# A hybrid decoder layer in one launch: another order of transfers, norms and splits in the opening

## The chip, the cores and the metric

The kernel runs on one core of a Trainium2 chip. Times are device microseconds (us) of that core for one execution of the whole program. The engines are named as in the profile: PE (TensorE, with its weight loads as PEld), ACT (ScalarE), DVE (VectorE), POOL (GpSimd) and SP (SyncE, which issues most of the transfers); "q" behind an engine's name is its sequencer or its DMA queue.

## The reference, cut to what matters

One layer over 512 tokens of width 1024, all in float32:

```
u    = rms_norm(x, attn_pre_norm)
proj = u @ w_in            # q, k, v, gate, beta, decay of group A; q, k, v of group B
mix  = concat(gated_delta_rule(...), block_attention(...)) @ w_out
h    = x + rms_norm(mix, attn_post_norm)
h    = h + rms_norm(relu(rms_norm(h, mlp_pre_norm) @ w_up)**2 @ w_down, mlp_post_norm)
out  = h + sigmoid(h @ w_ple_gate) * (p @ w_ple)
```

`p` is 512 x 256 and `w_ple` 256 x 1024. The change concerns the beginning: the product `p @ w_ple`, which depends on nothing else, the first norm, and the first product of `u`.

## The kernel before, in words

Tokens are tiled by 128 (four tiles, t = 0 to 3), the width by 128 as well (eight slices, k = 0 to 7). A float32 product is done as three products of the faster type float32r: every operand is split into a high part (a cast on ACT) and a low part (a subtraction on DVE), and `mm3` (L187 to L191) multiplies high by high, high by low and low by high. So each operand that comes from memory costs one transfer, one pass on ACT and one on DVE before PE can use it.

The opening runs, in the order of the source:

- Transfers of `p_in` (two halves, k = 0 and 1), of `wl_in` (w_ple in four pieces, from ACT's queue), of x tile 0 and of the identity (L124 to L130).
- Three products of a tile of zeros, `warm`, into `pwarm` (L132 to L136), and an ACTIVATE on one column of that tile (L137), the first one in the source, whose function needs the table load.
- Memsets of `half` and `root` on POOL, and `pad_l`, a tile that only takes up room (L146 to L150).
- The splits of `p` and of the first half of `wl` (`part_of`, L232 to L234), then `embed(0)` (L236 to L246): for k = 0, 1 and four token tiles one `mm3` each, 24 products in all, whose four results are copied out of PSUM as `pls` and stored to the DRAM tile `ple`, to be read at the very end of the kernel. The splits of the second half of `wl` follow (L247).
- The norm row `nw0`, from ACT's queue (L249), and the four loads of `wv`, the weight for the token-major projections, 256 rows x 520 columns each, split as they arrive (`load_chunk` and `load_w`, L158 to L177); the raw buffers are three, those of the high and low parts four. The loads of x tiles 1 to 3 stand between them (L251 to L257).
- For each token tile the norm (L261 to L270): a square with a running sum on ACT (L264), the root on POOL (L154, L155), the scaling to `u` on DVE (L267), eight transposes on PE into `ut` (L212) and their split into `uTh` and `uTl` (L203, L204). Behind tile 0 stands `embed(1)`, the other 24 products.

Then the pool `e` of the opening is closed, and the pool `g` of the next phase reuses its memory, each tile of it waiting for the tiles that it lies on. The `wv` products come next (L279 to L288): token tiles 0 and 1 in two column halves each, over k, then tiles 2 and 3, 192 products in all; `mov` and `ba` take their results. After them the first convolution product (`pc`, in `proj_conv`) and everything else follow.

The order in which an engine runs its instructions is not the order of the source alone: the build lays out each engine's list by rank, which is the place in the source, and by the time at which its own model has the operands ready. Each engine then works through its list strictly in order. Of the transfers issued from SP and ACT eight can be under way; the issue of a ninth waits for one to land.

## Time and profile before

| | |
|---|---|
| median of 3 runs | 696.66 us (695.54 to 699.62) |
| profiled execution, its own time | 695.17 us |
| its span in the trace | 693.4 us |
| PE busy | 678.2 us, 98% of the span |
| DVE, ACT, POOL busy | 438.6, 324.0, 48.7 us |
| moved by DMA | 79.24 MB, 114 GB/s on the mean |

A row of the trace tells when an instruction began and how long it lasted; in brackets stands the time for which its engine had been idle, and what ended that. A matmul's end is modelled, so the distance between two starts is the better measure of its cost. A transfer is shown by its issue; the time from there to landing stands in the list of transfers. The rows that the prediction uses stand in their own section below.

### The profile page before, as it was taken

To read this page: it belongs to the slowest core of one execution; us is meant where nothing else is said; L and a number is where in the kernel's file an instruction comes from. 1 tells how busy PE (TensorE), PEld (TensorE's weight loads), DVE (VectorE), ACT (ScalarE), POOL (GpSimd) and SP (SyncE) were. 2 spreads that over 40 slices of the span, in tenths; PEclk is the share of its full clock that TensorE was granted. 3 is DMA by queue.
4 is the path that set the end of the run, shared out by engine and by line. 5 is a ranking of instruction groups with operands and counts; after the bars stand their busy time and mean duration, and the time that the engine had idled before them with its cause. 6 is when DMAs were issued, how large, how long until landed. Compare 5 with 4: busy or idle time off the path is not lost.

```text
span 693.4 us, 9002 instructions
## 1 busy us (share of the span) xinstructions
PE 678.2 (98%) x3418; PEld 563.2 (81%) x3418; DVE 438.6 (63%) x687; ACT 324.0 (47%) x598; POOL 48.7 (7%) x91
## 2 busy tenths in 40 slices
PE   8999999999999999999999999999999999999897
PEld 5998888888877768789888888888888888688786
DVE  4748889367676656675385456956678758535532
ACT  6536343433466655545265644444435344523311
POOL 1401100000011100230000000000000000032100
PEclk9999999999999999999999999999999999999999
DMA  8731323532011118377004440154301123645521
GB/s 333 303 123 61 103 86 102 116 112 92 31 31 62 31 62 283 142 261 256 31 31 142 133 151 31 39 174 148 95 31 60 47 91 102 197 87 119 121 105 46
DMA packets 38556, 79.24 MB, mean 114 GB/s; under 512 B 9776, under 2 KB 10416, under 8 KB 38512
## 3 DMA queue, kind: packets, MB, share of 16 engines
q1 hardware_dynamic: 36640, 74.98, 32.8%
q0 software_dynamic: 1152, 2.10, 2.0%
q10 hardware_dynamic: 720, 1.57, 0.6%
q8 instruction: 27, 0.44, 0.3%
q14 instruction: 17, 0.14, 0.1%
HBM read 70.51 MB, written 7.08 MB: 112 GB/s over the span
## 4 chain that ended last, share of the span: by engine, by line
PE 85%; DMA 6%; ACT 3%; DVE 3%; issue 1%; POOL 1%; ACTq 0%; DVEq 0%; POOLq 0%
PE pu L191 16%; PE pd L191 13%; PE pu L188 8%; PE pd L188 7%; PE pc L191 6%; PE po L191 4%; PE pg L191 3%; PE pc L188 3%; PE pmk L191 2%; PE pmq L191 2%; PE po L188 2%; PE wv L191 2%; PE pz L191 2%; PE pg L188 2%; DMA sf<-in_w_down 1%
## 5 line engine op out<-in xcount | busy, mean ns | idle before, releaser
L191 PE MATMUL pd<-sr,sr 128*128 128x512 f32 x464 | 143.6, 390 | 0.8 <-DVE sr L682 0.8
L191 PE MATMUL pu<-u2Tl,sr 128*128 128x512 f32 (+1 forms) x288 | 105.3, 366 | 0.4 <-DVE u2Tl L204 0.4
L188 PE MATMUL pu<-u2Th,sr 128*128 128x512 f32 (+1 forms) x288 | 105.4, 366 | 0.0
L191 PE MATMUL pu<-u2Th,sr 128*128 128x512 f32 (+1 forms) x288 | 105.2, 365 | 0.0
L191 PEld LDWEIGHTS pd<-sr,sr 128*128 128x128 f32 x464 | 86.9, 188 | 19.9 <-DVE sr L682 1.9
L188 PE MATMUL pd<-sr,sr 128*128 128x512 f32 x232 | 90.7, 391 | 0.3 <-ACT sr L681 0.3
L682 DVE TENSOR_TENSOR sr<-sf,sr 128x1024 fp32r<-128x1024 f32 x48 | 58.5, 1221 | 37.6 <-ACT sr L681 13.9
L682 DVE TENSOR_TENSOR sr<-wd,sr 128x1024 fp32r<-128x1024 f32 x42 | 51.2, 1221 | 29.6 <-PE pu L191 28.2
L777 ACT ACTIVATE f<-pu 128x512 f32<-128x512 f32 (+1 forms) x36 | 19.9, 551 | 96.1 <-PE pu L191 96.1
L681 ACT CAST sr<-sf 128x1024 fp32r<-128x1024 f32 x48 | 50.2, 1047 | 25.6 <-DMA sf<-in_w_ple_gate 10.8
L191 PEld LDWEIGHTS pu<-u2Tl,sr 128*128 128x128 f32 x288 | 54.3, 189 | 9.4 <-DVE u2Tl L204 0.6
L191 PEld LDWEIGHTS pu<-u2Th,sr 128*128 128x128 f32 x288 | 54.3, 189 | 8.7
L188 PEld LDWEIGHTS pu<-u2Th,sr 128*128 128x128 f32 x288 | 54.3, 189 | 8.7
L681 ACT CAST sr<-wd 128x1024 fp32r<-128x1024 f32 x42 | 44.1, 1051 | 19.4 <-PE pd L191 19.4
L188 PEld LDWEIGHTS pd<-sr,sr 128*128 128x128 f32 x232 | 43.6, 188 | 9.8 <-ACT sr L681 1.0
L188 PE MATMUL pc<-uTh,w_h 128*128 128x512 f32 x96 | 39.0, 407 | 0.0
L191 PE MATMUL pc<-uTh,w_l 128*128 128x512 f32 x96 | 38.4, 400 | 0.0
L191 PE MATMUL pc<-uTl,w_h 128*128 128x512 f32 x96 | 38.2, 398 | 0.0
L832 DVE TENSOR_TENSOR sf<-sf,pd 128x512 f32<-128x512 f32 x28 | 19.1, 683 | 22.2 <-PE pd L191 22.2
L837 DVE TENSOR_TENSOR wd<-wd,wd 128x1024 f32<-128x1024 f32 x24 | 29.3, 1222 | 0.6
L188 PE MATMUL pg<-sr,h2Th 128*128 128x512 f32 (+1 forms) x72 | 26.5, 368 | 0.0
L191 PE MATMUL pg<-sr,h2Th 128*128 128x512 f32 (+1 forms) x72 | 26.3, 366 | 0.0
(421 smaller groups left out, 1319.8 us busy)
## 6 DMA issues: line engine op xcount, KB each, us to landing
sf<-in_w_up SPq DMA_DIRECT2D x32, 512.0 KB, 3.3
wd<-in_w_down SPq DMA_DIRECT2D x24, 512.0 KB, 4.4
w_r<-in_w_in SPq DMA_DIRECT2D x12, 512.0 KB, 3.6
wo_r<-in_w_out SPq DMA_DIRECT2D x8, 512.0 KB, 3.8
sf<-in_w_ple_gate SPq DMA_DIRECT2D x8, 512.0 KB, 4.3
sf<-in_w_down SPq DMA_DIRECT2D x8, 512.0 KB, 4.3
wv_r<-in_w_tok SPq DMA_DIRECT2D x4, 520.0 KB, 6.5
x<-in_x SPq DMA_DIRECT2D x4, 512.0 KB, 6.8
```

Source lines behind the costliest of these rows:

```text
L188: nc.tensor.matmul(dst, l[0], r[0], start=start, stop=False)
L191: nc.tensor.matmul(dst, a, b, start=False, stop=stop and i == 1)
L681: nc.scalar.copy(hi, src)
L682: nc.vector.tensor_sub(lo, src, hi.bitcast(F32))
L777: nc.scalar.activation(fq[:, side, c0:c1], pt[:, :n], AF.Relu)
L832: add(dst, dst, pts[j])
L837: sub(B[dst + (kk,)], B[x_ + (kk,)], B[y_ + (kk,)])
```

## The change

It rewrites the opening and leaves the rest as it is:

- The third product of zeros covers 128 columns instead of 512.
- The ACTIVATE for the table load works on a tile of its own, `first`, that POOL sets to zero; `pad_l` is gone.
- `nw0` and x tile 1 are loaded from POOL's queue, at the head of the kernel.
- The loads of `wv` are parted from their splits (`load_raw`, `split_raw`). Three loads are issued first, then x tiles 2 and 3; the fourth load comes behind the first split, because the raw buffers are three.
- The ranks are: norm of tile 0, `embed(1)`, norm of tile 1, split of wv0, load of wv3, `sm`, `kc`, the stores of `pls`, splits of wv1 and wv2, norm of tile 2, split of wv3, norm of tile 3. The stores of `pls`, so far beside each copy, come in one loop; its copies alternate between ACT and DVE.

```diff
-LEFT_PAD, RIGHT_PAD = 8, 56
+RIGHT_PAD = 56
...
+    nc.gpsimd.dma_start(nw0, norms[0:1, :].to_broadcast([P, D]))
+    nc.gpsimd.dma_start(x_h[1], x[P:2 * P, :])
...
-    for _ in range(3):
-        nc.tensor.matmul(pw, warm[:, :P], warm, start=True, stop=True)
-    nc.scalar.activation(warm[:, 0:1], warm[:, 0:1], AF.Square)
+    for n in (512, 512, P):
+        nc.tensor.matmul(pw[:, :n], warm[:, :P], warm[:, :n], start=True, stop=True)
+    first = cp.tile([P, 1], F32, name="first")
+    nc.gpsimd.memset(first, 0.0)
+    nc.scalar.activation(first, first, AF.Square)
...
-    cp.tile([P, LEFT_PAD], F32, name="pad_l")
...
-    def load_w(src, k0, nk, cols, name):
+    def load_raw(src, k0, nk, cols, name):
+        raw = wp.tile([P, 1040], F32, tag="raw", bufs=3, name=f"{name}_r")
+
+        nc.sync.dma_start(raw[:, :nk * cols].rearrange("p (k c) -> p k c", k=nk),
+                          src if len(src.shape) == 3 else src[k0 * P:(k0 + nk) * P, :].rearrange("(k p) c -> p k c", p=P))
+        return raw
+
+    def split_raw(raw, nk, cols, name):
...
+    def load_w(src, k0, nk, cols, name):
+        return split_raw(load_raw(src, k0, nk, cols, name), nk, cols, name)
...
-            (nc.vector.tensor_copy if t == 3 else nc.scalar.copy)(s, pts[t])
-            nc.sync.dma_start(ple[i, tk(t), :], s)
+            (nc.scalar.copy, nc.vector.tensor_copy)[t % 2](s, pts[t])
+            pls.append((i, t, s))
...
-    nc.scalar.dma_start(nw0, norms[0:1, :].to_broadcast([P, D]))
-    wv = []
-    for t in range(NT):
-        wv += load_chunk(w_tok[t * 256:(t + 1) * 256, :], 520, f"wv{t}", nk=2)
-        if t == 0:
-            load_x(1)
-        if t == 1:
-            load_x(2)
-            load_x(3)
-    nc.sync.dma_start(sm, small)
-    nc.sync.dma_start(kc, consts[:, P:])
-
-    for t in range(NT):
+    raw_v = [load_raw(w_tok, 2 * i, 2, 520, f"wv{i}") for i in range(3)]
+    load_x(2)
+    load_x(3)
+
+    def norm_in(t):
...
-        if t == 0:
-            embed(1)
+    wv = []
+
+    def split_v(i):
+        hi, lo = split_raw(raw_v[i], 2, 520, f"wv{i}")
+        wv.extend((hi[:, j, :], lo[:, j, :]) for j in range(2))
+    norm_in(0)
+    embed(1)
+    norm_in(1)
+    split_v(0)
+    raw_v.append(load_raw(w_tok, 6, 2, 520, "wv3"))
+    nc.sync.dma_start(sm, small)
+    nc.sync.dma_start(kc, consts[:, P:])
+    for i, t, s in pls:
+        nc.sync.dma_start(ple[i, tk(t), :], s)
+    for i in (1, 2):
+        split_v(i)
+    norm_in(2)
+    split_v(3)
+    norm_in(3)
```

## Rows read from the trace of the kernel before

**Rows 1.** The page, busy time, share of the span and instructions of each engine.

```profile
PE 678.2 (98%) x3418; PEld 563.2 (81%) x3418; DVE 438.6 (63%) x687; ACT 324.0 (47%) x598; POOL 48.7 (7%) x91
```

**Rows 2.** Busy time of each engine in two stretches, the opening and the rest: start and end, length, then busy us and instructions of each engine, the granted clock, the DMA share and GB/s.

```profile
0.00:46.40 46.40, 43.29 (x279) 37.54 (x280) 26.14 (x34) 25.66 (x45) 9.38 (x19) 1.00 0.69 261
46.40:693.40 647.00, 634.95 (x3141) 525.66 (x3139) 412.49 (x654) 298.36 (x554) 39.32 (x72) 1.00 0.33 104
```

**Rows 3.** The chain of work that ended last, in order of time, in its first 80 us: start, length, engine, tile and line.

```profile
1.16 5.31 DMA wl_in<-in_w_ple
6.49 6.68 DMA wv_r<-in_w_tok
13.19 1.06 ACT wv_h L166
14.25 1.06 ACT u L264 x2
...
16.26 1.30 DVE u L267
...
66.35 0.89 PE pkk L389 x8
```

**Rows 4.** PE's instructions in order of time, from the start to the first product behind the opening.

```profile
1.44 5.26 PE L136 MATMUL pwarm<-warm 128*128 128x512 f32 x6 [1.44 <-DVE warm L133]
5.95 0.99 PE L188 MATMUL pl<-wlh,pTh 128*128 128x512 f32 x1
...
7.01 0.39 PE L188 MATMUL pl<-wlh,pTh 128*128 128x512 f32 x1
...
16.09 0.39 PE L188 MATMUL pl<-wlh,pTh 128*128 128x512 f32 x1
17.60 1.09 PE L212 MATMUL ut<-ident,u 128*128 128x128 f32 x8 [1.12 <-DVE u L267]
...
20.21 0.66 PE L212 MATMUL ut<-ident,u 128*128 128x128 f32 x4 [0.35 <-DVE uTl L204]
20.62 0.37 PE L188 MATMUL wv<-wv_h,uTh 128*128 128x260 f32 x1
...
26.09 0.66 PE L212 MATMUL ut<-ident,u 128*128 128x128 f32 x4 [0.19 <-DVE uTl L204]
...
46.25 0.39 PE L188 MATMUL pc<-uTh,w_h 128*128 128x512 f32 x1
```

**Rows 5.** ACT's instructions and its queue's issues in order of time.

```profile
2.61 1.28 ACT L229 ACT_TABLE_LOAD   x1 [2.61 <-issue]
4.67 0.61 ACT L229 CAST wlh<-wl_in 128x512 fp32r<-128x512 f32 x1
6.75 0.20 ACT L137 ACTIVATE warm<-warm 128x1 f32<-128x1 f32 x1 [1.46 <-PE pwarm L136]
...
9.43 0.33 ACTq L249 DMA_DIRECT2D nw<-in_norms  x1
...
30.36 0.21 ACT L312 ACTIVATE ea<-sm 128x4 f32<-128x4 f32 x1
34.14 0.37 ACT L287 COPY mov<-wv 128x252 f32<-128x252 f32 x1 [3.57 <-DVE ba L286]
...
37.75 1.05 ACT L166 CAST w_h<-w_r 128x1024 fp32r<-128x1024 f32 x1 [2.25 <-PE wv L191]
```

**Rows 6.** Transfers issued in the first 45 us: tile and source, queue, count, size of one, median us from issue to landing.

```profile
wv_r<-in_w_tok SPq DMA_DIRECT2D x4, 520.0 KB, 6.5
x<-in_x SPq DMA_DIRECT2D x4, 512.0 KB, 6.8
ple<-pls SPq DMA_DIRECT2D x8, 256.0 KB, 5.9
...
nw<-in_norms ACTq DMA_DIRECT2D x1, 512.0 KB, 6.3
```

**Rows 7.** POOL's instructions late in the kernel, where it issues transfers: the first pair.

```profile
614.42 1.99 POOL L906 DMA_DIRECT2D sf<-hd  x2 [1.11 <-DVE sf L905]
```

**Rows 8.** Busy time in the stretch of the pl products, columns as in rows 2.

```profile
6.70:16.40 9.70, 9.70 (x44) 7.73 (x42) 5.91 (x8) 8.21 (x15) 0.75 (x2) 1.00 1.04 413
```

**Rows 9.** For whom SP's queue waited in the first 45 us: us in total, times, longest.

```profile
SPq L164 <- DMA wl_in<-in_w_ple: 2.9, 2, 1.8
...
SPq L121 <- DMA wl_in<-in_w_ple: 1.6, 1, 1.6
```

**Rows 10.** Groups of instructions of the first 46.4 us: line, engine, operation, shapes and count, then busy us and mean ns of one, then the idle time before them.

```profile
L204 DVE TENSOR_TENSOR uTl<-ut,uTh 128x512 fp32r<-128x512 f32 x8 | 5.2, 685 | 0.8 <-ACT uTh L203 0.8
L267 DVE SCALAR_TENSOR_TENSOR u<-x,r,nw 128x1024 f32<-128x1024 f32 x4 | 5.1, 1282 | 2.0 <-POOL r L155 2.0
L167 DVE TENSOR_TENSOR wv_l<-wv_r,wv_h 128x1040 fp32r<-128x1040 f32 x4 | 4.9, 1239 | 1.7 <-ACT wv_h L166 1.7
...
L244 DVE COPY pls<-pl 128x512 f32<-128x512 f32 x2 | 1.4, 682 | 0.0
```

**Rows 11.** SP's issues in order of time.

```profile
17.61 4.08 SPq L245 DMA_DIRECT2D ple<-pls  x4
21.74 4.05 SPq L164 DMA_DIRECT2D w_r<-in_w_in  x3
```

More of the change, by code (lines that the diff above doesn't have):

```diff
@@ L155, in rsqrt @@
         nc.gpsimd.tensor_tensor(dst, dst, half[:, :n], op=ALU.pow)
-    def load_w(src, k0, nk, cols, name):
+    def load_raw(src, k0, nk, cols, name):
[4 more added lines that the diff above has]
+    def split_raw(raw, nk, cols, name):
         n = nk * cols
-        raw = wp.tile([P, 1040], F32, tag="raw", bufs=3, name=f"{name}_r")
         hi = wp.tile([P, 1088], F32R, tag="hi", bufs=4, name=f"{name}_h")
         lo = wp.tile([P, 1088], F32R, tag="lo", bufs=4, name=f"{name}_l")
-        nc.sync.dma_start(raw[:, :n].rearrange("p (k c) -> p k c", k=nk),
-                          src if len(src.shape) == 3 else src[k0 * P:(k0 + nk) * P, :].rearrange("(k p) c -> p k c", p=P))
         nc.scalar.copy(hi[:, :n], raw[:, :n])
@@ L243, in embed @@
             s = e.tile([P, 512], F32, tag="pl", bufs=8, name=f"pls{i}_{t}")
-            (nc.vector.tensor_copy if t == 3 else nc.scalar.copy)(s, pts[t])
-            nc.sync.dma_start(ple[i, tk(t), :], s)
+            (nc.scalar.copy, nc.vector.tensor_copy)[t % 2](s, pts[t])
+            pls.append((i, t, s))
+    pls = []
     embed(0)
```

## The prediction

> **What bounds the kernel now.** I read the busy line of the page first. The reader should see TensorE (PE) busy for 678.2 of 693.4 us [rows 1]. So an edit that takes nothing off PE's own work can return no more than PE's idle time. Two windows, cut where the wv products end and the first convolution product (pc) begins, give that idle time by stage: 46.40 - 43.29 = 3.1 us in the opening, of which 1.44 us lies before the first product, and 647.00 - 634.95 = 12.1 us in all the rest [rows 2]. The change touches the opening alone, so its direct gain is capped near 3 us: PE's idle time there, plus what is cut from the products of zeros, less what stays.
>
> Next the chain that ended last, for the opening [rows 3]. It runs: a wl transfer (to 6.47), the issue of wv's second transfer that had waited for it, that transfer (to 13.17), ScalarE's split of it (13.19), two squares of the norms behind it, GpSimd's root, VectorE's u (16.26 to 17.56), then the transposes. So the norms wait behind a wv split that the products need much later. On PE's own timeline [rows 4] that is the hole between the pl product at 16.09 and the transposes at 17.60, with 1.12 us of idle time written beside it; a second of 0.35 us stands before the next transposes (20.21); then the wv products run nearly without a break to the first pc product at 46.25. From 46.25 on PE is fed, so what the opening saves is passed on, and what it loses too.
>
> **The change part by part.**
>
> *Fewer products of zeros.* Six warm records take 5.26 us, 0.877 each, two to a product [rows 4]. The third product shrinks from 512 to 128 columns, which removes 384/512 of two records: 0.75 x 2 x 0.877 = 1.3 us. The warm-up then ends near 5.4 instead of 6.7. The first pl product needs ScalarE's cast of wl, which starts at 4.67 and lasts 0.61 [rows 5], so it can start near 5.4 to 5.5, where the old one was queued at 5.95 [rows 4] behind zeros that lasted to 6.7 and came through at about 6.4.
>
> Those earlier products are slow ones, though. Later in the trace eight plain float32 products of 128 columns take 0.89 us [rows 3], 0.111 each or 0.445 per 512 columns; the warm records take 0.877, twice that. So by duration PE works at the lower of its two levels (1.2 of 2.4 GHz) up to about 6.5 us, after 5 us of unbroken zeros, and from the pl product at 7.01 on the starts are 0.227 us apart, the higher level: (16.09 - 7.01) / 40 steps [rows 4]. The granted clock reads 1.00 in all windows [rows 2] and doesn't show this. If the rise stays at 6.5, the us from 5.5 to 6.5 goes on two to three products at half speed. So the third pl product (7.01 before) begins near 6.45: a gain of 0.55 us; bounds 0 (nothing won) and 0.9 (5.5 against 6.4, all at the higher level).
>
> The Trainium skill (TensorE: Matmul & The Clock Gate, Part 1: The HAM clock gate) says the low level is the default, that sustained activity lifts it, and that the moment shifts between runs of one kernel. It speaks against cutting the warm products; by it the gain here could be lost, and that is the third rival below.
>
> *Table preload on its own tile.* Before, that ACTIVATE wrote a column of the zeros' tile, so ScalarE stood 1.46 us until the products had read it [rows 5]. After, it waits only for a memset on GpSimd. The table load (1.28 us from 2.61) comes first either way [rows 5], so 0.2 us moves to about 3.9, into time in which ScalarE waited for p. The second half of p is then split up to 1.4 us earlier, which costs or gives PE nothing: embed(0)'s second half starts at 8.6. The tile takes the pad's place; nothing for that.
>
> *nw0 and x1 from GpSimd's queue.* Removed: one issue on ScalarE's queue, one on SP's. Before, the norm row was issued at 9.43, behind ScalarE's casts [rows 5], and took 6.3 us to land [rows 6], so 15.7: u of tile 0 at 16.26 could hardly have been earlier even with the square done. After, both are issued in the first 3 us: a GpSimd issue occupies it 1.0 us (two in 1.99 us) [rows 7], so nw0 leaves at about 1.7 and x1 at 2.7. What lies behind them on GpSimd: the memset for the preload (needed at 3.9) and two more, no cost. What they collide with: p, wl and x0. The opening moves 261 GB/s on the mean and some 413 between 6.7 and 16.4 [rows 2, 8], so another 1.05 MB is 2.5 us of transfer put among 2.1 MB. Bounds for x0, x1 and nw0: 8 us (x0's issue at 1.62 plus 6.8) and 12. If all of the 1.05 MB came first, wl's second k would land 2.5 us after 6.47 [rows 3], at 9.0, and be split by 10.3 (casts of 0.6 and 0.7), while the 15th product wants it at 9.2: a hole of 1.1 us; and embed(1), due at 11.4, would find its first half by 12.3, where it wants it at 11.9. If the new transfers share, neither shows. I take 0.1 us, kept inside the 0.55, with 1.5 as the end.
>
> The Trainium skill (DMA: Bandwidth & Descriptors, Issuing engines are not separate DMA queues) says that all queues end on the same 16 engines, so other issuers save issue time only. By that the move is worth 0.3 to 0.4 us an issue. The rows show more here: SP stood 2.9 + 1.6 us waiting for wl transfers to land before it could issue [rows 9], which two transfers fewer on these queues shorten.
>
> *Two norms ahead of wv's splits.* The instructions and their durations are the same [rows 10]; only ranks move. The build orders each engine's work itself, by rank and modelled readiness: the preload stands ahead of the casts in the source, yet runs after two of them [rows 5]. With x0 and nw0 in by 8 to 12, the square of tile 0 runs at 9 to 12 in place of 14.25. From its start to the end of u took 17.56 - 14.25 = 3.3 us [rows 3], so u0 is done at 12.3 to 15.3 and u1 one pass (1.28) later, 13.6 to 16.6, while PE has embed(1) until about 17. Both idle holes go.
>
> What is late next? PE itself: the last of 48 pl products ends at 6.45 + 46 x 0.227 = 16.9, plus 16 transposes at 0.109 (8 in about 0.87) and four switches of some 0.1: 19.0 for the first wv product, against 20.62. Or VectorE: behind u1 stand up to four uTl passes at 0.685 and wv's first low half at 1.24 [rows 10]: 16.6 + 4 x 0.685 + 1.24 = 20.6 at worst, and under 19 from the early u1 (13.6). I take 19.5, nearer the PE end, since u0's chain has two free us.
>
> From the first wv product to the first pc product took 46.25 - 20.62 = 25.63 us, with four transposes (0.44) in it that now lie before, and 0.19 of idle [rows 4]: 25.0 is left. 19.5 + 25.0 = 44.5: a gain of 1.75; bounds 2.25 (19.0) and 0.65 (20.6).
>
> *wv3's load.* It needs the buffer that wv0's splits free, so it goes out at 17.5 to 20.6, lands 6.5 us later [rows 6], and is split in 2.4 (1.06 + 1.24 and a hand-over [rows 3, 10]): 26.4 to 29.5. PE asks for it after 6 of 8 k: 72 products at 0.119 (25.0 less 16 transposes, over 192) = 8.6, plus a transposed tile: about 28.9. Cost 0 to 1, I take 0.25.
>
> *ple's stores and pls.* Eight stores move on SP's queue behind wv3's issue, sm and kc, ahead of the next w loads, which went out at 21.74 and are first cast at 37.75 [rows 5, 11]. That 16 us covers them. VectorE copies four pls tiles in place of two (0.68 each, in embed's time, when it waits); ScalarE two fewer.
>
> **Sum.** 1.75 - 0.25 = 1.5 us less. The profiled execution took 695.17 us (span 693.4 and 1.8 around it), so 693.7 on its scale; it lies 1.5 us under the median of 696.66, on whose scale I forecast 695.2.
>
> **The rivals.**
> *1. The feed stays late.* x0 or x1 lands at the late bound, ScalarE stands at its square with the transposed tiles' casts behind it, and the first wv product stays at 20 to 21. For it: ScalarE and VectorE run in order and the new transfers share 16 full engines. Against it: two us of slack. Gain 0.5 to -0.5: about 696.7.
> *2. Slower: the stores block the next pool.* The next pool reuses the opening's memory, so its first writers wait for the stores that read pls. One of them, ea, sat on ScalarE at 30.36, ahead of the mov copies at 34.14 that free PSUM for the second half of wv's products [rows 5]. The last store was issued by 21.7 and landed about 5.9 later [rows 6, 11]; now it goes out at 24 to 28 and lands at 30 to 34. PE needs the copies at 19.5 + 12.5 = 32. From a landing at 32 on every us costs PE one; a landing at 36 costs 4 less the 1.5 won: 699.2. Against it: stores ahead of w loads, and ea may lie on other memory.
> *3. The clock rises late.* With fewer zeros and a short hole before the first pl product the higher level could come later than 6.5. Products at half the pace lose half of the delay, so from 3 us of delay the gain is gone: 696.7. For it: the rise came only at the zeros' end. Against it: pl products keep PE occupied.
> *4. The build orders later work differently.* Ranks and times shift, so engines behind 46.25 may be laid out anew. PE has 12.1 us of idle time there [rows 2], and a loss has no such cap: I price it at 3 us better than the forecast, 692.2, or 5 worse, 700.2. Nothing in the profile says which.
>
> **How the numbers follow.** Forecast 0.50 (its own range 693.7 to 696.5); rival 1 0.15; rival 2 0.10; rival 3 0.05; rival 4 0.20, half each way. A measurement here tells about 0.5%, 3.5 us, from no change: 693.2 and 700.1. Faster by more: most of rival 4's better half (0.09) and a tail of the forecast (0.04), 0.13. Slower by more: half of rival 2 (0.05) and most of rival 4's worse half (0.08), 0.13. The rest is 0.74. The range for 8 in 10 runs from 691.8 to 699.3.
>
> **What would show it.** Right: warm records end near 5.4, no ScalarE idle before the preload, nw0 landed by 12, the square of tile 0 before the first wv cast, no PE idle between the pl products and the transposes, first wv product at 19 to 20, first pc product at 44.2 to 45.6. Wrong: pl starts 0.43 apart past 7 us (rival 3); ScalarE idle on x (rival 1) or before ea or mov (rival 2); a first pc product that is earlier by 1.5 with a span that isn't (rival 4).

## The result and the profile after

| | before | after |
|---|---|---|
| median of 11 runs each, same chip | 696.48 us (695.22 to 699.62) | 700.69 us (699.16 to 702.35) |
| ratio after to before, 95% interval | | 1.0052 (1.0038 to 1.0066) |
| profiled execution, its span | 695.17, 693.4 us | 702.35, 700.6 us |
| first pc product, the end of the opening | 46.25 us | 51.06 us |

The change costs 0.5%: some 3.6 us by the ratio, 4.2 between the medians; the forecast was 1.5 us less. The traces are of one execution each, of the kernel before a short one and of the changed kernel the longest, and lie 7.2 us apart. Where the time went shows on PE's own timeline of the changed kernel, to be laid beside [rows 4] (lines have shifted: pwarm L138, pl L197 and L200, ut L221):

```profile
1.44 4.21 PE L138 MATMUL pwarm<-warm 128*128 128x512 f32 x6 [1.44 <-DVE warm L135]
5.35 0.80 PE L197 MATMUL pl<-wlh,pTh 128*128 128x512 f32 x1
...
6.25 0.39 PE L197 MATMUL pl<-wlh,pTh 128*128 128x512 f32 x1
...
11.61 0.50 PE L197 MATMUL pl<-wlh,pTh 128*128 128x512 f32 x1 [0.19 <-ACT wlh L238]
...
12.67 0.40 PE L197 MATMUL pl<-wlh,pTh 128*128 128x512 f32 x1
17.23 1.97 PE L221 MATMUL ut<-ident,u 128*128 128x128 f32 x8 [4.16 <-DVE u L269]
...
19.42 0.63 PE L200 MATMUL pl<-wll,pTh 128*128 128x512 f32 x1
19.85 0.63 PE L197 MATMUL pl<-wlh,pTh 128*128 128x512 f32 x1
...
26.33 0.37 PE L197 MATMUL wv<-wv_h,uTh 128*128 128x260 f32 x1
```

The start is won as forecast: the third pl product comes at 6.25 instead of 7.01. Then PE runs only four products of embed(1), to 12.67, and stands 4.16 us at the transposes, which its list has 28 products in (43 before). Behind that hole the pl products start 0.43 us apart (19.42, 19.85), not 0.227. PE in windows, with the granted clock in the column behind the busy time:

```profile
13.00:17.20 4.20, 0.07 (x1) 0.90 1.05 419
17.20:23.20 6.00, 5.97 (x18) 0.50 0.78 279
23.20:51.00 27.80, 27.80 (x227) 1.00 0.49 169
```

From 17.20 to 23.20 the clock was at the lower of its two levels (1.2 of 2.4 GHz). It fell inside the hole, while PE waited (1.00 up to 16.30, 0.50 from 16.60 on). The ledger of the 4.8 us by which pc is late: hole 4.16 against 1.12 + 0.35 + 0.19 before [rows 4], 2.5 us; low clock 2.9 (the set of transposes to the next product 1.62 us instead of 0.85, ten steps of pl 4.38 instead of 2.3); embed(1)'s first four products 0.7 late on their casts; less 0.76 won at the start. That makes 5.3, 0.5 too much. About half of that lies behind the first wv product: from there to pc it took 24.73 us, where 25.63 less 0.19 of idle and four transposes (0.44) would be 25.0 (the transposes now run in fewer and larger sets). The rest I can't trace to one row.

What PE waits for is seen on ACT, to be laid beside [rows 5]:

```profile
10.94 0.62 ACT L238 CAST wlh<-wl_in 128x512 fp32r<-128x512 f32 x1 [3.53 <-DMA wl_in<-in_w_ple]
12.22 0.62 ACT L238 CAST wlh<-wl_in 128x512 fp32r<-128x512 f32 x1 [0.67 <-DMA wl_in<-in_w_ple]
12.75 1.05 ACT L266 ACTIVATE u<-x 128x1024 f32<-128x1024 f32 x1
...
13.80 1.04 ACT L266 ACTIVATE u<-x 128x1024 f32<-128x1024 f32 x1
...
14.84 0.56 ACT L253 COPY pls<-pl 128x512 f32<-128x512 f32 x1
```

These two casts ran at 8.51 and 9.43 before. Both squares of the norms stand behind them in ACT's list. The rest of the way to u is on POOL:

```profile
13.99 0.19 POOL L157 TENSOR_SCALAR r<-ss 128x1 f32<-128x1 f32 x1 [11.28 <-ACT u L266]
15.02 0.19 POOL L157 TENSOR_SCALAR r<-ss 128x1 f32<-128x1 f32 x1 [0.84 <-ACT u L266]
15.29 1.08 POOL L158 TENSOR_TENSOR r<-r,half 128x1 f32<-128x1 f32 x2
```

POOL's list has the first operation of tile 1's root ahead of the second of tile 0's; before, tile 0's two ran one behind the other (15.39 and 15.66). So u of tile 0 waits for the square of tile 1 too, about 1.0 us by an estimate (15.29 against 13.99 + 0.27), and is done at 17.17. That order is one us of the hole beside the late casts, and the runs with both transfers on POOL's queue and the new ranks all have it (e1, e3, e7, e17 to e20).

And the list of transfers, to landing, beside [rows 6]:

```profile
wv_r<-in_w_tok SPq DMA_DIRECT2D x3, 520.0 KB, 9.6
x<-in_x SPq DMA_DIRECT2D x3, 512.0 KB, 8.8
wl_in<-in_w_ple ACTq DMA_DIRECT2D x4, 256.0 KB, 7.3
...
nw<-in_norms POOLq DMA_DIRECT2D x1, 512.0 KB, 8.2
x<-in_x POOLq DMA_DIRECT2D x1, 512.0 KB, 9.6
```

The queues from 6 to 9 us (packets, MB, share of the 16 engines), first the kernel before, then the changed one; q1 is SP's queue, q10 ACT's, which carries w_ple alone here, q0 POOL's:

```profile
q1 hardware_dynamic: 348, 0.68, 59.0%
q10 hardware_dynamic: 285, 0.51, 44.6%
```

```profile
q1 hardware_dynamic: 118, 0.47, 40.6%
q0 software_dynamic: 123, 0.45, 39.7%
q10 hardware_dynamic: 103, 0.20, 17.6%
```

With a third queue at work w_ple got 0.20 MB in this stretch instead of 0.51. Part of that is SP's: its packets are of 4.0 KB here (0.47 MB / 118) and were of 2.0 KB (0.68 / 348).

Behind the opening nothing was laid out anew: the first products of the stages pc, pmk, pz, pu, pd and pg came 4.8 to 5.1 us late, all by the same shift. In this one execution the last stage (pg to the end) was another 2.1 us longer; the argument doesn't use it.

### The profile page after: what moved, and what is told of

Its sections match the earlier page's. It is cut to its first block, busy times and chain, and to the rows that moved or that the text cites. A ratio compares the mean times of both kernels' runs of the same rounds, so it can differ in the third digit from the quotient of the medians.

```text
span 700.6 us, 9007 instructions
## 1 busy us (share of the span) xinstructions
PE 681.7 (97%) x3418; PEld 566.5 (81%) x3418; DVE 438.7 (63%) x689; ACT 323.2 (46%) x596; POOL 49.4 (7%) x94
## 3 DMA queue, kind: packets, MB, share of 16 engines
q10 hardware_dynamic: 576, 1.05, 0.4%
## 4 chain that ended last, share of the span: by engine, by line
PE 90%; DMA 4%; DVE 2%; ACT 2%; issue 1%; POOL 1%; ACTq 0%
PE pu L200 15%; PE pd L200 14%; PE pu L197 8%; PE pd L197 7%; PE pc L200 6%; PE pg L200 4%; PE po L200 4%; PE pc L197 3%; PE wv L200 2%; PE pg L197 2%; PE pmk L200 2%; PE pmq L200 2%; PE po L197 2%; PE pz L200 2%; DMA sf<-in_w_down 1%; DMA wl_in<-in_w_ple 1%
## 5 line engine op out<-in xcount | busy, mean ns | idle before, releaser
L200 PE MATMUL pd<-sr,sr 128*128 128x512 f32 x464 | 143.4, 390 | 0.9 <-DVE sr L701 0.9
L200 PE MATMUL pu<-u2Tl,sr 128*128 128x512 f32 (+1 forms) x288 | 105.4, 366 | 0.8 <-DVE u2Tl L213 0.8
L197 PE MATMUL pu<-u2Th,sr 128*128 128x512 f32 (+1 forms) x288 | 105.4, 366 | 0.0
L200 PE MATMUL pu<-u2Th,sr 128*128 128x512 f32 (+1 forms) x288 | 105.2, 365 | 0.0
L200 PEld LDWEIGHTS pd<-sr,sr 128*128 128x128 f32 x464 | 86.9, 188 | 19.9 <-DVE sr L701 2.0
L197 PE MATMUL pd<-sr,sr 128*128 128x512 f32 x232 | 90.7, 391 | 0.3 <-ACT sr L700 0.3
L700 ACT CAST sr<-sf 128x1024 fp32r<-128x1024 f32 x48 | 50.3, 1048 | 26.7 <-DMA sf<-in_w_ple_gate 11.1
L200 PEld LDWEIGHTS pu<-u2Tl,sr 128*128 128x128 f32 x288 | 54.3, 189 | 9.6 <-DVE u2Tl L213 1.0
L200 PEld LDWEIGHTS pu<-u2Th,sr 128*128 128x128 f32 x288 | 54.3, 189 | 8.8
L197 PEld LDWEIGHTS pu<-u2Th,sr 128*128 128x128 f32 x288 | 54.3, 189 | 8.8
L197 PEld LDWEIGHTS pd<-sr,sr 128*128 128x128 f32 x232 | 43.6, 188 | 9.8 <-ACT sr L700 1.0
L197 PE MATMUL pc<-uTh,w_h 128*128 128x512 f32 x96 | 39.0, 407 | 0.0
L200 PE MATMUL pc<-uTh,w_l 128*128 128x512 f32 x96 | 38.4, 400 | 0.0
L200 PE MATMUL pc<-uTl,w_h 128*128 128x512 f32 x96 | 38.2, 398 | 0.0
L200 PE MATMUL pg<-sr,h2Tl 128*128 128x512 f32 (+1 forms) x72 | 27.0, 376 | 0.0
L200 PE MATMUL pg<-sr,h2Th 128*128 128x512 f32 (+1 forms) x72 | 27.0, 375 | 0.0
```

Of the source, the lines that this page charges most:

```text
L197: nc.tensor.matmul(dst, l[0], r[0], start=start, stop=False)
L200: nc.tensor.matmul(dst, a, b, start=False, stop=stop and i == 1)
L700: nc.scalar.copy(hi, src)
```

## The experiments

All ratios are to the kernel before on the same chip. "Hole" is the longest idle time of PE in the opening behind its first product, "first pc" is the first pc product; both are from the one profiled execution of each run, the ratio from all of them.

| run | ratio (95% interval) | hole, us | first pc, us |
|---|---|---|---|
| the change | 1.0052 (1.0038 to 1.0066) | 4.16 | 51.06 |
| e1 embed(1) first | 1.0065 (1.0042 to 1.0087) | 2.79 | 51.13 |
| e2 old queues | 1.0088 (1.0053 to 1.0123) | 5.97 | 50.72 |
| e3 POOL's transfers later | 1.0142 (1.0108 to 1.0177) | 8.02 | 55.11 |
| e4 before, with POOL's queue | 1.0059 (1.0032 to 1.0086) | 2.75 | 50.11 |
| e5 only the row from POOL | 1.0033 (1.0011 to 1.0054) | 3.31 | 48.17 |
| e6 row and x1 from SP | 1.0015 (0.9995 to 1.0035) | 2.45 | 47.19 |
| e7 zeros in the hole | 1.0072 (1.0046 to 1.0097) | 1.34 | 51.18 |
| e8 before, zeros and preload | 1.0000 (0.9985 to 1.0015) | 2.48 | 47.57 |
| e9 as e6, embed(1) first | 1.0020 (0.9998 to 1.0042) | 1.93 | 47.27 |
| e15 before, row earlier | 1.0003 (0.9986 to 1.0020) | 0.72 | 47.23 |
| e17 w_ple from SP | 1.0025 (1.0001 to 1.0050) | 1.61 | 47.86 |
| e18 POOL in halves | 1.0063 (1.0038 to 1.0089) | 4.77 | 51.18 |
| e19 w_ple by whole rows | 1.0013 (0.9983 to 1.0042) | 0.88 | 46.40 |
| e20 one row block whole | 1.0039 (1.0020 to 1.0058) | 3.40 | 50.81 |

### Which part costs: e1 to e4

My first theory was that PE's list is at fault (transposes 28 products in). e1 ranks embed(1) ahead, the rest as changed:

```diff
-    norm_in(0)
     embed(1)
+    norm_in(0)
```

> The changed kernel with one rank altered: embed(1) stands ahead of the norm of tile 0. In the build's list for PE all 48 pl products now come before the first transposes (28 in the changed kernel, 43 in the kernel before). Theory (list order): PE has the second embed to run while wl's late pieces hold up ScalarE, so the hole of 4.2 us before the transposes shrinks below 1 us, the clock stays at 1.00 there, and the first pc product comes at 45 to 47 in place of 51.1; time 0.997 to 1.003 of before. Rival (late feed): the transposes come no earlier, since u is done at 17.2 all the same, and everything behind waits for it: first pc product past 48, time above 1.003.

```profile
15.56 0.50 PE L197 MATMUL pl<-wlh,pTh 128*128 128x512 f32 x1 [2.16 <-ACT pls L253]
...
24.39 1.12 PE L221 MATMUL ut<-ident,u 128*128 128x128 f32 x4 [2.79 <-DVE uTl L213]
```

PE's list had all 48 products first, and the loss stayed. The hole moved to PSUM tiles that ACT's copies free (they stand behind the late casts and the two squares) and to uTl, which VectorE works off behind three halves of wv. The clock stayed at 1.00 to 23 us and was low only about the second of these holes (0.62 from 23 to 27). The theory of the list alone fell.

e2 puts both transfers back on their old queues and keeps the new ranks:

```diff
-    nc.gpsimd.dma_start(nw0, norms[0:1, :].to_broadcast([P, D]))
-    nc.gpsimd.dma_start(x_h[1], x[P:2 * P, :])
...
+    nc.scalar.dma_start(nw0, norms[0:1, :].to_broadcast([P, D]))
...
+        if i == 0:
+            load_x(1)
```

> The changed kernel with the norm row back on ScalarE's queue and x tile 1 back on SP's, each at its old place; ranks as changed. PE's list has 30 pl products before the first transposes. Theory (list order): wl lands at 8.5 and 9.4 again, but the norm row, issued near 9.5, lands near 16, u of tile 0 is done near 17.3, and PE stands before the transposes from about 13 on: a hole of 3 to 4.5 us, a low clock after it, time 1.002 to 1.007 of before. Rival (the transfers from GpSimd's queue are the whole cause): no hole, time 0.996 to 1.001.

w_ple's casts were back at 8.43 and 9.28, but the norm row, issued at 9.29 and 7.5 us on its way, held u of tile 0 until 18.2: a hole of 5.97. The new ranks need an early norm row.

e3 holds POOL's two transfers until w_ple has landed, by a copy of one column of it into both tiles:

```diff
+    for dst in (nw0, x_h[1]):
+        nc.gpsimd.tensor_copy(dst[:, 0:1], wl_in[:, 1, D - 1:D])
     nc.gpsimd.dma_start(nw0, norms[0:1, :].to_broadcast([P, D]))
```

> The changed kernel, but both transfers from GpSimd's queue are issued only when the last piece of wl has landed (a copy of one element of it into their targets goes first). PE's list has all 48 pl products before the first transposes. Theory (what counts is when they are issued and what PE's list holds, not which queue): wl's pieces land near 8.5 and 9.4, the pl products end near 17, the norm row lands near 15 to 16, a hole of at most 1.5 us, no low clock; first pc product at 45 to 47, time 0.997 to 1.002. Rival (a transfer from GpSimd's queue is slow in itself): it lands 9 us or more after its issue, the transposes come past 20, time above 1.003.

The casts were early (8.57, 9.40), but ACT then stood 6.32 us at x tile 1. The square of tile 0 was done at 11.1 and the norm row in by 17.0; u of tile 0 began at 24.34 all the same, since POOL's list has tile 1's first operation ahead of tile 0's second (20.32), and VectorE's list has two wv halves ahead of u, whose casts stand behind the square of tile 1. Worse than either theory had it: that square is as much a head-of-line wait as the casts.

e4 is the kernel before, with only the two transfers moved to POOL's queue:

```diff
+    nc.gpsimd.dma_start(nw0, norms[0:1, :].to_broadcast([P, D]))
+    nc.gpsimd.dma_start(x_h[1], x[P:2 * P, :])
...
-    nc.scalar.dma_start(nw0, norms[0:1, :].to_broadcast([P, D]))
...
-            load_x(1)
```

> The kernel before with one part of the change: the norm row and x tile 1 from GpSimd's queue at the head. PE's list has 36 pl products before the first transposes, in place of 43; ScalarE's list has wl's late casts, a wv cast and three copies before the square of tile 0. Theory (late wl plus list order): wl's last pieces are cast at about 11 and 12.2, u of tile 0 is done near 18, PE stands 2.5 to 4 us before the transposes, time 1.002 to 1.008 of before. Rival (the queue is harmless, the ranks did it): hole of about 1 us as before, time 0.997 to 1.002.

```profile
9.87 0.62 ACT L231 CAST wlh<-wl_in 128x512 fp32r<-128x512 f32 x1 [2.27 <-DMA wl_in<-in_w_ple]
...
11.85 0.62 ACT L231 CAST wlh<-wl_in 128x512 fp32r<-128x512 f32 x1 [1.35 <-DMA wl_in<-in_w_ple]
```

```profile
15.93 0.80 PE L190 MATMUL pl<-wlh,pTh 128*128 128x512 f32 x1 [2.75 <-ACT pls L246]
```

With the old ranks the move to the third queue alone makes a loss as large as the change's (by the ratio; by the first pc product 3.9 of 4.8 us). The hole lies ahead of a pl product here: its PSUM tile is freed by ACT's copies (15.29), which stand behind the late casts and two wv casts.

### The dose, the place, the clock: e5 to e8

e5 leaves only the norm row on POOL's queue; x tile 1 goes back to SP, behind wv0.

```diff
-    nc.gpsimd.dma_start(x_h[1], x[P:2 * P, :])
...
+        if i == 0:
+            load_x(1)
```

> The changed kernel, but tile 1 of x goes back to SyncE's queue, behind the first pair of wv; of the two GpSimd transfers only the norm row (0.52 MB instead of 1.05 MB) is left. Theory of shares (every megabyte on a third queue in the first 12 us is taken from the pieces of w_ple): the last cast of w_ple, at 10.94 and 12.22 us in the changed kernel and at 8.51 and 9.43 in the kernel before, comes about half way back, at 9.5 to 11.5; tile 1 of x now lands later, at 15 to 18 us, and its square stands behind it on ScalarE. The hole ahead of the first transposes is 1.5 to 4 us and the ratio to the kernel before 1.000 to 1.005. Rival, it is a third queue as such that costs, whatever its bytes: casts at 10.9 and 12.2 as in the changed kernel, hole of 4 us and more, ratio 1.005 to 1.008.

Casts at 9.89 and 10.78, about half way back, as the theory of shares had it for half the bytes. Hole 3.31, ratio 1.0033, with an interval that reaches into the change's. The loss is not a clean dose: POOL ran tile 0's root without waiting for tile 1 here (12.54, 12.81), PE's list had 24 products ahead of the transposes, and the profiled execution took 696.70 where the median of the ten is 699.92.

e6 puts both on SP's queue behind the identity, ahead of wv:

```diff
+    nc.sync.dma_start(nw0, norms[0:1, :].to_broadcast([P, D]))
+    load_x(1)
...
-    nc.gpsimd.dma_start(nw0, norms[0:1, :].to_broadcast([P, D]))
-    nc.gpsimd.dma_start(x_h[1], x[P:2 * P, :])
```

> The changed kernel, with nothing on GpSimd's queue: the norm row and tile 1 of x are issued on SyncE's, behind the unit matrix and ahead of the first pair of wv. Two queues carry everything, as in the kernel before, but the norm row comes 3 places earlier than wv. Theory of shares: w_ple's last casts are back at 8.4 to 9.5 us, the norm row lands at 10 to 12 us, the first transposes stand 0 to 1.5 us ahead of their operand, TensorE's clock stays at its high level, the first pc product is at 45 to 47 us (46.25 before, 51.0 changed) and the ratio is 0.997 to 1.001. Rival, the new order of the ranks is what costs (transposes 24 products in instead of 43, the norms' squares ahead of the PSUM copies on ScalarE): a hole of 2.5 us or more is left ahead of the transposes or ahead of embed(1), the clock falls, the first pc product comes past 48.5 and the ratio is over 1.003.

```profile
13.79 1.10 PE L221 MATMUL ut<-ident,u 128*128 128x128 f32 x8 [2.45 <-DVE u L269]
```

Casts at 8.75 and 9.81, and ACT's queue moved 0.53 MB from 6 to 9 us, as before the change (0.51). Most of the loss is gone with the same bytes loaded nearly as early (the norm row landed at 10.8 instead of 9.5), and the interval lies below the change's. POOL's wait for tile 1 is gone as well (11.58, 11.85), so the whole gain isn't that of the casts. What is left is the list's part: the transposes stand 24 products in, and u isn't ready then. The hole was larger than the theory had it (0 to 1.5).

e7 fills the hole of the changed kernel with products of zeros:

```diff
+        if t == 0:
+            pf = ptr("pfill")
+            for _ in range(5):
+                nc.tensor.matmul(pf, warm[:, :P], warm, start=True, stop=True)
         transpose_in(u, uT, t, "ut")
```

> The changed kernel with 5 more products of zeros (float32, 512 columns, a PSUM tile of their own that nothing reads), ranked ahead of tile 0's transposes: 4 of them fall in the hole of 4.2 us, 1 ahead of the first pl product. The feed is left as late as it is; only TensorE's idleness goes. Theory, the hole costs twice, once as a wait for u and once as a low clock behind it (20 products at 427 ns instead of 230 and a set of transposes at half speed, 2.8 us): the granted clock stays above 0.9 from 17 to 23 us, the first pc product comes 2 to 3 us sooner than in the changed kernel (51.0), at 48 to 49.5, and the ratio is 1.001 to 1.004. Rival, the products after the hole are held by other waits anyway (PSUM copies, casts behind the squares), so that a high clock there buys nothing: first pc product at 50.5 or later, ratio 1.004 to 1.008.

```profile
17.33 1.06 PE L221 MATMUL ut<-ident,u 128*128 128x128 f32 x8 [1.34 <-issue]
...
24.50 0.37 PE L197 MATMUL wv<-wv_h,uTh 128*128 128x260 f32 x1
...
26.28 0.62 PE L197 MATMUL wv<-wv_h,uTh 128*128 128x260 f32 x3 [0.82 <-ACT uTh L212]
```

Two of the five products ran ahead of the first pl product (7.39 instead of 5.35) and three in the hole. The granted clock stayed at 1.00 and the first wv product came 1.83 us sooner (24.50 for 26.33). All of it was given back: PE waited for uTh and uTl, the build's list had the next transposes in smaller sets, and pc began at 51.18. So keeping the clock did not bring the ledger's 2.9 us back here. But PE's list differed (24 pl products ahead of the transposes, not 28), so that the clock has no price of its own isn't shown, and the record of all executions speaks against it: of the 31 of the kernel before that were timed beside e5 to e8, the seven with a mean granted clock of 0.999 or more took 695.9 us on the mean, the ten with 0.996 or less 698.6 (the eleven of the changed kernel had 0.991 to 0.997). A longer wait may lie behind both the clock and the time there.

e8 is the kernel before with only the short third product of zeros and the preload on its own tile (the first two parts of the diff).

> The kernel before, with only the first two parts of the change: the third product of zeros over 128 columns instead of 512, and the table preload on a tile of its own in place of the pad. Queues and ranks stay. Theory: the first pl products start 0.76 us sooner, as in the changed kernel, and the clock rises sooner by some tenths, but the transposes wait for u as before, so most of it goes into the idle ahead of them (1.12 and 0.35 us before): first pc product 45.5 to 46.3 us, ratio 0.998 to 1.001. Rival, fewer products of zeros leave TensorE idler in the first microseconds and the clock rises later, or the hole ahead of the transposes grows past the point where the clock falls: first pc product past 47, ratio 1.002 to 1.006, and then this part has a share in the loss.

The third pl product came at 6.03, 0.98 sooner than before, and PE stood 2.48 us ahead of the transposes instead of 1.12; u of tile 0 was 0.45 later there, the clock fell behind the hole, and the first pc product came at 47.57, past the 47 of the rival. The 12 runs say 1.0000 (0.9985 to 1.0015), as the theory had it: these two parts neither cost nor give.

### Can the idle time be had at all: e9, e15, e17

e9 is e6 with embed(1) ranked ahead of the norms.

> The kernel of the run with the norm row and tile 1 of x on SyncE's queue, and embed(1) ranked ahead of norm_in(0) as well, so that the transposes stand 48 products in and not 24. There TensorE stood 2.45 us ahead of the transposes, from 10.95 to 13.79 us, with 24 ready products behind them. Theory, with a punctual feed that hole is only the place in TensorE's list: it goes, and a smaller one comes at embed(1)'s third PSUM tile, which ScalarE's first copy (13.1 to 13.6 us, behind two squares) frees: 0.4 to 1.2 us. First wv product 17.5 to 19.5 us (20.98 there), first pc product 44.5 to 46.3 (47.2 there), ratio to the kernel before 0.997 to 1.000. Rival, the squares ahead of the copies and the three wv splits ahead of the uTl on VectorE hold TensorE just as long, as in the earlier run with embed(1) first (holes of 2.16 and 2.79 us): first pc product at 47 or later, ratio 1.001 to 1.004.

```profile
21.90 0.66 PE L221 MATMUL ut<-ident,u 128*128 128x128 f32 x4 [1.93 <-DVE uTl L213]
```

```profile
16.51 3.54 DVE L173 TENSOR_TENSOR wv_l<-wv_r,wv_h 128x1040 fp32r<-128x1040 f32 x3
...
21.16 1.28 DVE L213 TENSOR_TENSOR uTl<-ut,uTh 128x512 fp32r<-128x512 f32 x2
```

All 48 products ran with 0.18 us of idle, the first wv product came at 19.46 instead of 20.62, where the prediction had wanted it. Then PE stood 1.93 us for uTl, behind three halves of wv on VectorE (3.54 us). First pc 47.27. The rival took it.

e15 goes from the kernel before: short zeros, preload tile, embed(1) ahead of all norms, and the norm row on SP between wv0 and x tile 1:

```diff
     for t in range(NT):
         wv += load_chunk(w_tok[t * 256:(t + 1) * 256, :], 520, f"wv{t}", nk=2)
         if t == 0:
+            nc.sync.dma_start(nw0, norms[0:1, :].to_broadcast([P, D]))
             load_x(1)
```

> The kernel before with the short product of zeros and the preload tile, the norm row moved from ScalarE's queue to SyncE's between the first pair of wv and tile 1 of x, and embed(1) ahead of the norms of all tiles. Nothing on GpSimd's queue. ScalarE's list is then: last casts of w_ple, first wv cast, square of tile 0, three PSUM copies, square of tile 1. Theory: w_ple lands as in the kernel before (casts at 8.5 to 9.9 us), the norm row some 3 us sooner (12 to 13 us instead of 15.7), u of tile 0 is done at 15 to 15.5 and no longer ends last; the transposes follow the 48 products without idle at 16.5 to 17.5, with at most 1 us of idle ahead of a PSUM tile; first pc product 44.5 to 46 us (46.25 before), ratio 0.997 to 1.000. Rival, the copies or the second tile's u take the place of the wait removed: idle of 1.5 us and more stays, first pc product past 46.3, ratio 1.000 to 1.003.

u of tile 0 was done at 14.9 and the transposes came at 17.5 without idle, but PE stood 0.60 us at a PSUM tile ahead of them, and 0.58, 0.72 and 0.48 us at uTl behind them. First pc 47.23, ratio 1.0003.

e17 keeps POOL's queue and moves w_ple's late pieces to SP, ahead of x tile 0:

```diff
+    for k in range(2):
+        nc.sync.dma_start(wl_in[:, k, 512:D], w_ple[k * P:(k + 1) * P, 512:D])
     load_x(0)
     nc.sync.dma_start(ident, consts[:, K_ID:K_ID + P])
-    for k in range(2):
-        nc.scalar.dma_start(wl_in[:, k, 512:D], w_ple[k * P:(k + 1) * P, 512:D])
```

> The changed kernel, with the two late pieces of w_ple taken from ScalarE's queue and issued on SyncE's, behind p and ahead of tile 0 of x; the norm row and tile 1 of x stay on GpSimd's queue. Theory (the third queue costs by the share that it takes from w_ple's late pieces, which ScalarE waits for in order): with the pieces early, the casts are at 7.5 to 10 us in spite of GpSimd's queue (10.94 and 12.22 in the changed kernel), and tile 0 of x and the unit matrix land later, so that its square is at 10.5 to 12.5. The hole ahead of the transposes is at most 2 us instead of 4.2, TensorE's clock stays high, first pc product 46 to 48.5 (51.0 changed), ratio 0.999 to 1.003. Rival, a third queue slows every transfer and what is late merely changes: holes of over 3 us in the first 25 us, first pc product past 49, ratio over 1.004.

Casts at 8.86 and 10.54, largest hole 1.61, pc at 47.86: by the middle value about half of the loss is back while POOL's queue stays. But PE's list had 44 products ahead of the transposes, and u of tile 0 came later than in the changed kernel (19.28), behind two wv halves on VectorE. So this run doesn't part w_ple's lateness from the list; e19 does.

### Why a third queue takes so much: e18 to e20

From 6 to 9 us the three queues of the changed kernel moved 118, 123 and 103 packets, but 0.47, 0.45 and 0.20 MB. Equal turns by packet would do that: w_ple's packets are of 2 KB (half a row), the others near 4 KB. e18 cuts POOL's transfers into halves of 512 columns:

```diff
+    for c in (slice(0, 512), slice(512, D)):
+        nc.gpsimd.dma_start(nw0[:, c], norms[0:1, c].to_broadcast([P, 512]))
+    for c in (slice(0, 512), slice(512, D)):
+        nc.gpsimd.dma_start(x_h[1][:, c], x[P:2 * P, c])
```

> The changed kernel, with the norm row and tile 1 of x on GpSimd's queue each cut into two transfers of 512 columns, so that their packets are 2 KB instead of 4 KB. Nothing else moves. Theory: the queues take turns by packet, not by byte. In the changed kernel they moved 118 (SyncE), 103 (ScalarE) and 123 (GpSimd) packets from 6 to 9 us, but 0.47, 0.20 and 0.45 MB, since only ScalarE's (w_ple) are of 2 KB. With GpSimd's at 2 KB the counts stay about equal, at 120 to 150 each, and the bytes become about 0.55, 0.28 and 0.28 MB; w_ple's last cast moves from 12.22 us to 11.2 to 11.8. Tile 1 of x lands later for that, at 13 to 15.5, and its square stands ahead of the PSUM copies, so the time gains little: ratio 1.003 to 1.008. Rival, the engines are shared by bytes or by issues: ScalarE's queue keeps 0.18 to 0.22 MB in that stretch, the casts stay at 10.9 and 12.2.

```profile
q0 software_dynamic: 133, 0.46, 47.1%
q1 hardware_dynamic: 124, 0.47, 39.7%
q10 hardware_dynamic: 129, 0.25, 21.2%
```

The counts are equal again, but POOL's packets stayed at 0.46 MB / 133 = 3.5 KB (in all 320 packets for 1.05 MB, where the changed kernel has 288): on this queue a packet isn't a row, so the edit didn't change what it was meant to. Casts at 10.43 and 12.36. By itself it doesn't tell the theories apart.

e19 loads w_ple by whole rows, in two transfers with packets of 4 KB:

```diff
-        nc.scalar.dma_start(wl_in[:, k, 0:512], w_ple[k * P:(k + 1) * P, 0:512])
+        nc.scalar.dma_start(wl_in[:, k], w_ple[k * P:(k + 1) * P, :])
...
-    for k in range(2):
-        nc.scalar.dma_start(wl_in[:, k, 512:D], w_ple[k * P:(k + 1) * P, 512:D])
```

> The changed kernel, with w_ple loaded by whole rows: two transfers of 512 KB with packets of 4 KB on ScalarE's queue, in place of four of 256 KB with 2 KB. GpSimd's queue keeps the norm row and tile 1 of x. Theory of turns by packet: from 6 to 9 us the three queues move about equal counts again, but ScalarE's has 0.3 to 0.4 MB (0.20 in the changed kernel), so the casts of w_ple's late half are at 8 to 10 us instead of 10.94 and 12.22, in spite of the third queue. The first pl product comes 0.5 to 1.2 us later (5.35 in the changed kernel), since the first 512 KB must land and p, still of 2 KB packets, gives way; tile 0 of x lands at 10.5 to 12. The hole ahead of the transposes is 1 to 2.5 us instead of 4.16, the clock stays high or falls for less long, first pc product 47.5 to 49.5 (51.06), ratio 1.001 to 1.005. Rival, a third queue takes its share whatever the packets: the casts stay past 10.5, first pc product past 50, ratio 1.005 to 1.009.

```profile
q10 hardware_dynamic: 184, 0.69, 57.5%
q1 hardware_dynamic: 215, 0.41, 37.8%
q0 software_dynamic: 17, 0.07, 5.6%
```

```profile
15.30 1.09 PE L219 MATMUL ut<-ident,u 128*128 128x128 f32 x8 [0.25 <-DVE u L267]
```

The first fence is of 3 to 6 us: ACT's queue moved 0.69 MB there (0.42 in the changed kernel) with somewhat fewer packets than SP's, so all but 0.24 MB of w_ple was in when POOL's queue came up. Casts from 9.08 to 10.7, hole 0.25, no idle at all from there to pc at 46.4. The first product came 1.2 us later (6.53), as expected. Ratio 1.0013 (0.9983 to 1.0042): by its middle value three quarters of the change's loss are gone, and no loss at all lies within the interval. POOL's queue, the ranks and the bytes are as changed, and so are PE's list (28 products ahead of the transposes) and POOL's wait for tile 1 (13.09, 13.36): what differs is how w_ple arrives. This is the run that shows the cause: the ratio's interval still overlaps the change's a little, the holes (0.25 and 4.16) don't, and e18, with the same list and timed beside it, has 1.0063.

e20 wants both, the early start and the early casts:

```diff
+    nc.scalar.dma_start(wl_in[:, 0, 0:512], w_ple[0:P, 0:512])
+    nc.scalar.dma_start(wl_in[:, 1], w_ple[P:2 * P, :])
+    nc.scalar.dma_start(wl_in[:, 0, 512:D], w_ple[0:P, 512:D])
```

> The changed kernel, with w_ple in three transfers: first the first half of the first 128 rows (2 KB packets, as it was), then the second 128 rows whole (4 KB), then the rest (2 KB). It should keep the early start of the changed kernel (first pl product at 5.35; 6.53 with whole rows throughout) and the early casts of the run with whole rows. Theory: casts of the late half at 9 to 10.7 us, hole ahead of the transposes 0 to 1.5 us, clock high, first pc product 45.2 to 46.8 (46.4 with whole rows, 46.25 before), ratio 0.998 to 1.001. Rival, the last piece, of 2 KB packets and last in line, is what the late half waits for again: casts past 10.9, hole over 2.5 us, ratio 1.003 and more.

```profile
q0 software_dynamic: 115, 0.46, 44.5%
q1 hardware_dynamic: 110, 0.44, 37.3%
q10 hardware_dynamic: 113, 0.23, 20.2%
```

```profile
17.16 1.97 PE L221 MATMUL ut<-ident,u 128*128 128x128 f32 x8 [3.40 <-DVE u L269]
```

```profile
11.64 1.14 ACT L238 CAST wlh<-wl_in 128x512 fp32r<-128x512 f32 x2 [3.23 <-DMA wl_in<-in_w_ple]
```

The rival was right. The fence is of 6 to 9 us: the last piece, of 2 KB packets, got its 113 turns and 0.23 MB, and the casts waited for it until 11.64; the hole is back, in the same list. No version beat the kernel before: e6, e8, e9, e15 and e19 can't be told from it.

## Why the prediction was wrong

**What bounds it** was right: PE is the bound, the opening passes its shift on whole (4.8 to 5.1 us at every later stage).

**Fewer products of zeros**: 0.55 us forecast for the third pl product, 0.76 measured, inside 0 to 0.9. But e8 shows that by itself it moves no time: the hole ahead of the transposes grew.

**Preload on its own tile**: right. ACT has no idle ahead of it (3.91).

**nw0 and x1 from POOL's queue**: this is the step that failed. The bound was nearly right (w_ple at most 2.5 us later; 2.4 and 2.8 measured at the casts). But "if the new transfers share, neither shows. I take 0.1" chose the wrong end, and even the late end was priced by embed alone (1.1 us and 0.4), where embed lost only 0.7. The price was in what stands behind those casts in ACT's list: the squares (12.75 and 13.80), the PSUM copies, and through POOL's root and u the transposes: a hole of 4.16 us. The part had asked what the transfers collide with, and not who queues behind the one that loses.

The Trainium skill's rule cited there (DMA: Bandwidth & Descriptors, Issuing engines are not separate DMA queues: all queues end on the same 16 engines) agrees with the trace: the shares of the three queues add up to 98%. Its second half, that another issuer saves issue time only, doesn't: with the same ranks the same bytes made the ratio 1.0015 from SP's queue (e6) and 1.0052 from POOL's. Another rule of the Trainium skill bore on this step and was missed: DMA: Bandwidth & Descriptors, Queues, rings and completion order, says that each engine goes round the queues it has work for, one packet at a time. The counts agree (118, 103, 123 in the changed kernel; 133, 124, 129 in e18; 115, 110, 113 in e20). From the packet sizes alone, 2 KB beside 4 and 4, an estimate of w_ple's share would have been a fifth of the bytes; it had 0.20 of 1.12 MB, 18%.

**Two norms ahead**: "the square of tile 0 runs at 9 to 12" was wrong by the casts ahead of it (it ran at 12.75), though x tile 0 and the norm row were in by about 10.4 and 9.5 (issued at 1.62 and 1.26; 8.8 and 8.2 us to landing). The 3.3 us from its start to the end of u became 4.4, for POOL's root waited for the second square. The prediction had read [rows 3] as "two squares" ahead of the root; the x2 is one square and the reading of its sum (14.15 and 15.12), and the second square (15.20) held nothing there. "While PE has embed(1) until about 17" was wrong too: the rank that puts the norm ahead of embed(1) puts its transposes ahead as well, 28 products in and 24 in e6. With a punctual feed that leaves 2.45 us (e6). So "both idle holes go" had two causes of failure, and e1 and e6 each undo one of them. And where both are undone, in e9, "19.5" for the first wv product is met (19.46), while "25.0 is left" behind it is not: 27.8, for VectorE's wv halves come ahead of uTl. The prediction had named that end (up to 20.6) for the first wv product, but it bites behind it.

**wv3's load, the stores**: no price seen. wv3 was issued at 21.72, later than forecast, but PE stood nowhere in the wv stage. (The 0.119 per product there is 0.121 by its own sum, (25.0 - 16 x 0.109) / 192.) ea and mov ran 4.6 and 4.8 us later than in [rows 5], with the shift, so rival 2 did not happen.

**The rivals**: rival 1 (the feed stays late, ACT stands with everything behind it) had the right mechanism with the wrong transfer, w_ple and not x, and priced it at 1.5 us over the forecast, where the median came out 5.5 over it. Rival 3 had a late clock at the start; the clock rose early (pl starts 0.23 apart from 6.25 on) and fell in the hole. Rival 4 is excluded by the constant shift. None of the slower cases was this one, so 0.13 for slower was too little.

## What to carry to other kernels

When a load moves to another queue while the engines are full, work out for each transfer already under way what share it keeps, packet size counted, and then read what is queued in order behind the engine that waits for it: the loss is there, not at the transfer. An idle hole next to a tight list can be worth little: e9 and e15 each removed the one ahead of the transposes, and the next operand (uTl, a PSUM tile) took its place within 5 us. A build that orders by modelled landings lays out everything on that model; moving a rank or a transfer moves the operation's consumers on other engines too. Of these runs only e18, e19 and e20 kept the changed kernel's list on PE, and only they part the feed from the order.

## What the runs showed of the hardware, unexpected

- Three queues got about equal packet counts, not equal bytes, while all had work (6 to 9 us of the changed kernel, e7, e18 and e20, 103 to 133 each); the one with 2 KB packets had 0.20 to 0.25 MB in these 3 us beside two with 0.44 to 0.47. In e5, with half as much on POOL's queue, the counts were 141, 104 and 119.
- Rows cut in half made half as large packets on ACT's queue (0.51 MB / 285 = 1.8 KB), but not on POOL's (3.5 KB in e18, 3.7 in the changed kernel).
- A hole's length alone doesn't tell whether PE's clock falls: 3.31 us in e5 and 2.45 in e6 left it at 1.00; 2.48 in e8 and 3.40 in e20 did not (0.61 from 18 to 20 us, 0.52 from 17 to 23). Each is one execution, and executions of one kernel differ in their mean clock (the kernel before: 0.992 to 1.000). What decides stays open.
- Why the profiled execution of the changed kernel had another low stretch (0.57 from 661 to 665 us), behind a wait of 2.15 us that the kernel before has with 1.76, stays open too.
